# One core, a two-layer hybrid backbone: decay rows read back from memory by SP's queue, rotation by a shuffle, four heads' squares beside each other, modulation's sums as products of rounded parts

## The chip, the cores and the metric

The kernel runs on 1 core of one Trainium2 chip. The metric is the device time of one execution in microseconds (us). The engines are named as in the profile: PE is TensorE (matrix products; PEld its weight loads), DVE is VectorE, ACT is ScalarE, POOL is GpSimd, SP is SyncE, which here only issues DMAs.

## The reference

Two layers over 256 latent and 256 context tokens of 1024 channels, float32. Each layer modulates its input, runs two token mixers on one combined projection, and then a mixture of 16 experts. What the change touches, cut:

```python
m_lat = jnp.split(jax.nn.silu(c) @ mod_w[l] + mod_b[l], 6, axis=-1)      # shift, scale, gate, twice; m_ctx alike
...
def rope_2d(x, cos, sin):                 # on q and k of the attention branch, latent tokens
    x1, x2 = xs[..., 0, :], xs[..., 1, :]
    out = jnp.stack([x1 * c - x2 * s, x2 * c + x1 * s], axis=-2)
...
q = l2_normalize(q.reshape(B, L, G_HEADS, G_KEY_DIM))    # DeltaNet branch; k alike
...
gcum = jnp.cumsum(chunk3(g), axis=-1)     # g: log decay, per token, head and direction
decay = jnp.exp(jnp.where(causal, gcum[..., :, None] - gcum[..., None, :], -jnp.inf))
a_mat = jnp.where(strict, jnp.einsum('nbhid,nbhjd->nbhij', kb, kc) * decay, 0.0)
sol = lax.linalg.triangular_solve(a_mat + jnp.eye(CHUNK), rhs, ...)
qk = jnp.where(causal, jnp.einsum('nbhid,nbhjd->nbhij', qc, kc) * decay, 0.0)
```

## The kernel before

The program is written as some hundred strands (Python generators: `modulation`, `conv_worker`, `norms`, `build`, `double`, `scan`, `att_worker`, `attend`, the expert strands). A planner (`Scheduler`) takes one operation after the other from the strands, by costs written in the code and by a table of priorities (`PRIO`), and writes each engine's instructions in that order; on the chip each engine runs its list in order and waits on semaphores. All weight loads go through SP's list. Buffers come from pools: 20 pages (128 x 2048 numbers), 16 `t5` (128 x 512), 14 `tiny`, and the 8 PSUM banks. An operation that finds no buffer makes its strand wait.

The places that the change and the prediction's steps touch:

- Decay rows. `decay_gates` makes `GC`, the sums of the log decays, with the token on the partition. The difference of two sums needs a row as well: `grow` makes it by four transposes on PE (one for each head) of a column repeated 128 times, into a bank. `build(t)` needs such rows for each of 4 tiles and 2 directions to make A; `double(t, d)` inverts I + A by blocks (products of 32 x 32 and 64 x 64 pieces), and then needs the same rows again for P, the decayed products of q and k, in the place where A stood. `scan` waits for P by `p_ev`.
- Squares. Behind each head's short convolution, `conv_worker` squares the head (ACT) and sums over the 128 channels, which lie on the partitions, by one product with a column of ones for each tile, into `Y.sqs`, a bank held by the whole layer's DeltaNet branch. `norms` copies them out for the root.
- Rotation. In `att_worker` a product with a permutation matrix (`K["perm"]`) swaps each 16 rows with the next 16; then come two multiplications and an addition on DVE.
- Modulation. `modulation` multiplies SiLU(c) with 512 columns of weights in four groups of 32 rows of PE beside each other, and sums the four partial results by a product with a 0/1 matrix (`sel2`), in float32. For the gates and the second shift and scale (`kind >= 2`) that product is 2 x 512.

A product of float32 numbers stands in the trace as two records, one of numbers rounded to `F32R` as one, a transpose as one. A float32 weight matrix is used as a rounded part and the rest (`split`), in three products (`mm3`).

## Time and profile before

| | us |
|---|---|
| median of 3 runs (lowest, highest) | 1632.36 (1616.32, 1634.97) |
| the profiled execution | 1628.14 |
| its span, first to last instruction | 1626.0 |
| PE busy in it | 1493.8 |
| DVE busy | 931.7 |
| ACT busy | 535.8 |

The span falls into stretches: until about 600 us the dense part of the first layer (modulation, projections, DeltaNet, attention, merging), to about 960 its routing and experts, to about 1320 the dense part of the second layer, then routing and the experts of that layer. Every time below is counted from the start of the span. A busy share is read within one stretch; the granted clock of PE stands beside it as a share of full speed.

### The profile page before, as it was taken

How to read it: one execution, taken by the hardware profiler on the slowest of the kernel's cores; microseconds unless marked ns; L12 is line 12 of the kernel's file. 1: busy time of each engine (PE TensorE's matmuls, PEld its weight loads, DVE VectorE, ACT ScalarE, POOL GpSimd, SP SyncE). 2: the span in 40 equal slices, each digit the busy share in tenths (PEclk: the TensorE clock that was granted, in tenths of full speed). 3: DMA queues.
4: the chain of work that ended last, by engine and by line, in shares of the span. 5: the costliest groups of instructions: out<-in, count | busy, mean ns of one | idle time of the engine just before them, and what ended most of it. 6: DMA issues, size and time to landing. Idle time of an engine off the chain costs nothing. (4 is left out here: it accounts for less than half of the span.)

```text
span 1626.0 us, 24829 instructions
## 1 busy us (share of the span) xinstructions
PE 1493.8 (92%) x9551; PEld 1017.6 (63%) x9552; DVE 931.7 (57%) x2391; ACT 535.8 (33%) x950; POOL 63.1 (4%) x84
## 2 busy tenths in 40 slices
PE   5999999999999977999999899999999957999974
PEld 2776788756787843465564367788889844454421
DVE  1677945768437586365575966792778666210023
ACT  2533343434331121264553253343554302110110
POOL 1000000000000001111010000000000000000000
PEclk9999999999999997999998999996999977999988
DMA  9415522152336577799998743440055955899994
GB/s 312 158 53 175 160 57 80 50 210 91 117 130 249 190 302 283 277 422 403 417 383 326 260 151 109 156 102 5 28 182 176 312 218 214 304 421 421 420 408 203
DMA packets 147725, 363.17 MB, mean 223 GB/s; under 512 B 27932, under 2 KB 82284, under 8 KB 122256
## 3 DMA queue, kind: packets, MB, share of 16 engines
q1 hardware_dynamic: 139808, 342.91, 56.9%
q0 software_dynamic: 6512, 16.38, 3.0%
q10 hardware_dynamic: 1280, 2.23, 0.4%
q8 instruction: 77, 1.26, 0.3%
q14 instruction: 48, 0.39, 0.1%
HBM read 345.47 MB, written 21.56 MB: 226 GB/s over the span
## 5 line engine op out<-in xcount | busy, mean ns | idle before, releaser
L451 PE MATMUL bank<-page,page 128*128 128x512 f32 (+3 forms) x3776 | 733.7, 349 | 13.5 <-ACT page L485 6.5
L451 PEld LDWEIGHTS bank<-page,page 128*128 128x128 f32 (+2 forms) x3776 | 567.6, 189 | 126.1 <-issue 27.3
L489 DVE TENSOR_TENSOR page<-page,page 128x1024 fp32r<-128x1024 f32 (+3 forms) x219 | 250.8, 1164 | 96.9 <-ACT page L485 94.9
L485 ACT ACTIVATE page<-page 128x1024 fp32r<-128x1024 f32 (+1 forms) x196 | 200.3, 1046 | 122.8 <-PE bank L451 65.8
L463 PE MATMUL bank<-page,t 128*64 128x512 f32 (+2 forms) x736 | 208.9, 607 | 6.8 <-DMA page<-in_w_exp_dram 5.9
L485 ACT ACTIVATE t<-bank 128x512 f32<-128x512 f32 (+5 forms) x168 | 79.8, 480 | 306.7 <-PE bank L468 210.5
L489 DVE TENSOR_TENSOR t<-bank,t 128x512 f32<-128x512 f32 (+3 forms) x63 | 49.6, 792 | 188.0 <-PE bank L463 153.8
L485 ACT ACTIVATE page<-bank 128x512 f32<-128x512 f32 (+2 forms) x127 | 70.2, 557 | 222.1 <-PE bank L451 97.9
L463 PE MATMUL bank<-page,page 128*32 128x512 f32 (+2 forms) x512 | 136.0, 604 | 8.0 <-DMA page<-in_w_exp_dram 7.6
L463 PEld LDWEIGHTS bank<-page,t 128*64 128x64 f32 (+2 forms) x736 | 64.6, 147 | 103.4 <-issue 87.1
L451 PE MATMUL bank<-t,page 32*32 32x16 f32 (+4 forms) x1472 | 117.1, 244 | 2.1 <-DVE t L504 1.8
L451 PEld LDWEIGHTS bank<-t,page 128*128 128x128 f32 (+3 forms) x1472 | 104.9, 160 | 18.9 <-issue 11.3
L468 PE MATMUL bank<-cf,t 128*128 128x128 f32 (+2 forms) x468 | 79.1, 287 | 36.0 <-DVE t L489 25.9
L468 PEld LDWEIGHTS bank<-cf,t 128*128 128x128 f32 (+2 forms) x468 | 54.8, 144 | 70.6 <-DVE t L489 31.8
L463 PEld LDWEIGHTS bank<-page,page 128*32 128x32 f32 (+2 forms) x512 | 47.0, 144 | 81.2 <-issue 67.1
L451 PE MATMUL bank<-page,csil 128*32 128x512 f32 x384 | 68.0, 678 | 17.2 <-DMA page<-in_mod_w_dram 16.5
L451 PE MATMUL bank<-page,t 128*128 128x512 f32 (+2 forms) x392 | 81.4, 346 | 2.1 <-DVE page L489 1.1
L451 PEld LDWEIGHTS bank<-page,t 128*128 128x128 f32 (+1 forms) x392 | 56.0, 185 | 26.4 <-issue 9.2
L518 DVE SCALAR_TENSOR_TENSOR t<-bank,tiny,t 128x508 f32<-128x508 f32 (+3 forms) x96 | 66.5, 700 | 7.5 <-ACT t L480 6.4
L480 ACT ACTIVATE t<-bank,tiny 128x512 f32<-128x512 f32 (+1 forms) x72 | 44.6, 623 | 53.5 <-PE bank L451 27.8
L480 ACT ACTIVATE page<-page 128x512 f32<-128x512 f32 (+2 forms) x44 | 25.6, 588 | 84.1 <-DVE page L489 48.5
L468 PE MATMUL bank<-cf,page 128*128 128x128 f32 (+1 forms) x248 | 41.7, 305 | 9.9 <-DMA page<-h_dram,cd 8.4
(178 smaller groups left out, 1139.7 us busy)
## 6 DMA issues: line engine op xcount, KB each, us to landing
page<-in_w_exp_dram SPq DMA_DIRECT2D x192, 1024.0 KB
page<-in_mod_w_dram SPq DMA_DIRECT2D x48, 1024.0 KB
page<-in_w_in_dram SPq DMA_DIRECT2D x44, 1024.0 KB
page<-in_w_o_dram SPq DMA_DIRECT2D x8, 1024.0 KB
y_dram<-t POOLq DMA_DIRECT2D x6, 1024.0 KB, 8.3
page<-m_dram SPq DMA_DIRECT2D x12, 512.0 KB
page<-y_dram SPq DMA_DIRECT2D x6, 1024.0 KB
page<-in_w_pb_dram SPq DMA_DIRECT2D x4, 1024.0 KB
```

The lines of the kernel that those rows point to most:

```text
L451: lambda: PE.matmul(o, a, b, start=start, stop=stop, skip_group_check=True))], [o], [a, b])
L463: PE.matmul(o, a, b, start=start, stop=stop, skip_group_check=True)
L468: SC.rec([("PE", 0.11, lambda: PE.transpose(o, a, idn))], [o], [a])
L480: SC.rec([("ACT", acte(width(o), in_psum(a)), lambda: S.activation(o, a, f, bias=bias, scale=scale, **k))], aps(o, accum_out), aps(a, bias ...
L485: SC.rec([("ACT", acte(width(o), in_psum(a)), lambda: S.activation(o, a, AF.Copy, bias=0.0, scale=1.0)), ("DVE", dve(width(o), in_psum(a), ...
L489: opts = [("DVE", dve(width(o), in_psum(a) or in_psum(b)), lambda: V.tensor_tensor(out=o, in0=a, in1=b, op=op)), ("POOL", 0.1 + width(o) * ...
L518: lambda: V.scalar_tensor_tensor(o, a, s, b, op0=op0, op1=op1, **k))],
```

## The change

In `build`, the rows of the sums come from memory: `decay_gates` transposes `GC` once, copies it and writes it to `gc_dram` (32 x 128 numbers); for every two tiles one DMA reads all 16 rows back into the page of A, each to all 128 partitions. For P, `double` reads the four rows of a tile and direction again, into the place of A, once it is done with A (`sum_rows`), and a strand of its own, `decayed`, makes P from them. `conv_worker` keeps its squared head in a `t5`; `norms` multiplies a 128 x 32 block of ones with the squares of four heads, each on 32 columns of PE's array beside the others, copies the bank, and brings the sums to tokens by a product with a 0/1 matrix for each tile. The rotation swaps rows by DVE's shuffle. The sums of modulation with `kind >= 2` are two products of rounded parts with a 0/1 matrix of 16 columns.

```diff
@@ modulation
-            cpy(part, bk)
+            if kind < 2:
+                cpy(part, bk)
+            else:
+                lo_ = yield "t5"
+                split(pt_.r(512), lo_.r(512), bk)
...
-                mm(bk[:2, :], K["sel2"], part, True, True)
-                tt(part[:2, :], bk[:2, :], br, OP.add)
-                dma(m_dram[l, :, i * 512:(i + 1) * 512], part[:2, :], "ACT")
+                mm(bk[:16, :], sel2r, pt_.r(512), True, False)
+                mm(bk[:16, :], sel2r, lo_.r(512), False, True)
+                tt(br, bk[:2, :], br, OP.add)
+                SC.free(lo_)
+                dma(m_dram[l, :, i * 512:(i + 1) * 512], br, "ACT")
@@ conv_worker
                 act(a4, dst, AF.Square)
-                for t in range(2 * ns):
-                    mm(Y.sqs[:, 1 - part, 2 * s0 + t, hd:hd + 1], a4[:, t, :], ones[:, 0:1], True, True)
+                Y.sq[part, hd] = a_
@@ norms
+        b = yield "bank"
+        n0 = 256 if Y.last and part == 0 else 0
+        mm_beside([b.v(512)[32 * hd:32 * hd + 32, n0:] for hd in range(4)], [ones[:, :32]] * 4,
+                  [Y.sq[part, hd].v(512)[:, n0:] for hd in range(4)], True, True)
+        st = yield "t5"
+        cpy(st.v(512)[:, n0:], b.v(512)[:, n0:])
+        SC.free(b, *(Y.sq.pop((part, hd)) for hd in range(4)))
+        w, w2, b = yield ("tiny", "tiny", "bank")
...
+        for t in range(n0 // 128, 4):
+            mm(b.v(4, 16)[:, t], st.v(4, 128)[:, t], K["selH"], True, True)
+        vcopy(shaped(sq, (4 - n0 // 128, 4)), b.v(4, 16)[:, n0 // 128:, :4])
@@ decay_gates
+        b, rows_ = yield ("bank", "t5")
+        tr(b.v(128)[:32], gv[:, 6, :])
+        cpy(rows_.v(128)[:32], b.v(128)[:32])
+        dma(dram(gc_dram[l], 0, [[128, 32], [1, 128]]), rows_.v(128)[:32])
+        SC.free(b, rows_)
@@ in place of grow
+    def sum_rows(Y, t, d):
+        dma(cell(Y.pA, t, d).rearrange("p h j -> p (h j)"),
+            dram(gc_dram[Y.l], (t * 8 + d * 4) * 128, [[0, 128], [1, 512]]))
@@ build
+        if t % 2 == 0:
+            dma(Y.pA[si].v(2048), dram(gc_dram[Y.l], si * 2048, [[0, 128], [1, 2048]]))
+            SC.set(Y.gc_ev[si])
+        yield Y.gc_ev[si]
...
-            A = cell(Y.pA, t, d)
-            b = yield "bank"
-            gr = grow(Y, b, t, d)
+            A = gr = cell(Y.pA, t, d)
@@ double, behind the inverse
-                b = yield "bank"
-                gr = grow(Y, b, t, d)
...
+                sum_rows(Y, t, d)
+    def decayed(Y, groups):
+        for t, d in groups:
+            if t not in Y.tiles:
+                continue
+            yield Y.u_ev[t, d]
+            for hd in range(4):
+                yield Y.conv_ev[0, hd]
+            A = cell(Y.pA, t, d)
+            for hd in range(4):
+                stt(A[:, hd], A[:, hd], hcol(Y.GC, t, d, hd), capP[:, d], OP.subtract, OP.min)
...
@@ att_worker
-                b = yield "bank"
-                mm(b.v(256), K["perm"], lat, True, True)
-                tt(tmp.v(256), b.v(256), K["sin"], OP.mult)
-                SC.free(b)
-                tt(lat, lat, K["cos"], OP.mult)
-                tt(lat, lat, tmp.v(256), OP.add)
+                SC.rec([("DVE", dve(256, False), lambda o=tmp.v(256), a=lat:
+                         V.stream_shuffle(out=o, in_=a, mask=[c ^ 16 for c in range(32)]))], [tmp.v(256)], [lat])
+                tt(tmp.v(256), tmp.v(256), K["sin"], OP.mult)
+                tt(tmp.v(256, o=256), lat, K["cos"], OP.mult)
+                tt(lat, tmp.v(256, o=256), tmp.v(256), OP.add)
```

The table of priorities stays as it was (`decayed` takes the one of its `double`, plus 0.01). Since the planner works on the new list of operations, the order changes all over. Three places, in the first layer. First SP's list ahead of the first pieces of A that are written out (`blk_dram`); before:

```order
L537 DMA page_317<-in_mod_w_dram 128x4x512
L537 DMA page_800<-in_mod_w_dram 128x4x512
L537 DMA page_1028<-in_mod_w_dram 128x4x512
L537 DMA page_1045<-in_mod_w_dram 128x4x512
L537 DMA page_1083<-in_w_in_dram 128x8x256
L537 DMA page_1097<-in_mod_w_dram 128x4x512
L537 DMA page_1102<-in_mod_w_dram 128x4x512
L537 DMA blk_dram<-page_934 16x16x16 x3
```

The same place of SP's list now:

```order
L538 DMA page_322<-in_mod_w_dram 128x4x512
L538 DMA page_747<-in_mod_w_dram 128x4x512
L538 DMA gc_dram<-t_852 32x128
L538 DMA page_884<-gc_dram 128x2048
L538 DMA page_886<-gc_dram 128x2048
L538 DMA page_910<-in_mod_w_dram 128x4x512
L538 DMA page_1026<-in_mod_w_dram 128x4x512
L538 DMA blk_dram<-page_884 16x16x16 x8
```

The write of the sums and the two reads of 1 MB stand between two loads of modulation weights; the second read, and all behind it, comes after the write has landed.

Further on in SP's list, where the block inverses of the first layer are done, before:

```order
L537 DMA page_1536<-in_w_in_dram 128x8x256
L537 DMA page_1547<-in_w_in_dram 128x8x256
L537 DMA page_1589<-in_mod_w_dram 128x4x512
L537 DMA t_1636<-inv_dram 16x16x16 x2
L537 DMA page_1701<-in_mod_w_dram 128x4x512
```

And there now, with the rows for P (each `page<-gc_dram 128x512` waits for the last product that reads A of its tile and direction):

```order
L538 DMA page_1647<-in_w_in_dram 128x8x256
L538 DMA page_1659<-in_w_in_dram 128x8x256
L538 DMA page_884<-gc_dram 128x512
L538 DMA page_1692<-in_mod_w_dram 128x4x512
L538 DMA page_884<-gc_dram 128x512
L538 DMA page_1848<-in_mod_w_dram 128x4x512
L538 DMA page_884<-gc_dram 128x512
L538 DMA page_1944<-in_w_in_dram 128x8x256
L538 DMA page_884<-gc_dram 128x512
L538 DMA page_886<-gc_dram 128x512 x3
L538 DMA page_2730<-in_mod_w_dram 128x4x512
```

Eight such reads stand among the weight loads, each ahead of the next load.

Last PE's list where `double` works on tiles 2 and 3 of the first layer (the pieces of 32x16, 64x32 and 32x32 are `double`'s, those of 128x256 an attention projection's), before:

```order
L451 MATMUL bank_2518<-t_2448,page_936 128x128 x4
L451 MATMUL bank_2527<-t_2517,page_936 32x16 x16
L451 MATMUL bank_2432<-page_2342,page_115 128x256 x2
L451 MATMUL bank_2432<-page_2342,page_117 128x256
L451 MATMUL bank_2432<-page_2342,page_115 128x256 x2
L451 MATMUL bank_2554<-t_2517,t_1636 32x16 x16
L451 MATMUL bank_2432<-page_2342,page_117 128x256
L451 MATMUL bank_2391<-t_2265,t_1636 32x16 x13
L451 MATMUL bank_2415<-page_2250,page_114 128x256 x2
L451 MATMUL bank_2587<-t_2517,page_936 64x32 x8
```

And now:

```order
L452 MATMUL bank_2214<-t_2205,page_886 32x16 x16
L452 MATMUL bank_2217<-t_2203,page_886 32x16 x16
L452 MATMUL bank_2245<-t_2205,t_1370 32x16 x16
L452 MATMUL bank_2265<-t_2203,t_1370 32x16 x16
L452 MATMUL bank_2275<-page_1649,page_118 128x256 x2
L452 MATMUL bank_2285<-t_2205,page_886 64x32 x8
L452 MATMUL bank_2299<-t_2203,page_886 64x32 x8
L452 MATMUL bank_2275<-page_1649,page_120 128x256
L452 MATMUL bank_2275<-page_1649,page_118 128x256 x2
L452 MATMUL bank_2323<-t_2205,t_1370 32x32 x8
```

Both directions run at once, and fewer products of the projection stand between their small pieces.

## Rows read from the trace of the kernel before

**Rows 1.** The page: busy us of each engine, share of the span, instructions.

```profile
PE 1493.8 (92%) x9551; PEld 1017.6 (63%) x9552; DVE 931.7 (57%) x2391; ACT 535.8 (33%) x950; POOL 63.1 (4%) x84
```

**Rows 2.** Windows by stretch: length, busy of PE, PEld, DVE, ACT, POOL, clock, DMA share, GB/s.

```profile
40.00:600.00 560.00, 544.66 (x3867) 418.25 (x3860) 364.14 (x944) 199.78 (x386) 12.50 (x18) 0.99 0.42 140
...
640.00:960.00 320.00, 302.22 (x1363) 167.04 (x1361) 199.93 (x380) 139.42 (x189) 25.48 (x27) 0.96 0.86 336
960.00:1320.00 360.00, 351.15 (x3032) 299.29 (x3032) 244.08 (x624) 144.72 (x282) 6.71 (x12) 0.95 0.45 148
...
1360.00:1600.00 240.00, 226.78 (x973) 97.17 (x973) 48.65 (x155) 32.30 (x55) 6.98 (x7) 0.98 0.97 395
```

**Rows 3.** Groups of instructions by form, PE: removed kinds (busy us, mean ns, idle before).

```profile
L468 PE MATMUL bank<-cf,t 128*128 128x128 f32 x456 | 77.2, 288 | 29.6 <-DVE t L489 25.9 <-DVE t L518 2.0 <-DVE tiny L518 1.2
...
L451 PE MATMUL bank<-t,cf 128*2 128x512 f32 x32 | 16.3, 592 | 2.4 <-ACT t L485 2.4
...
L451 PE MATMUL bank<-ones,t 128*128 128x1 f32 x112 | 13.8, 242 | 0.2 <-ACT t L480 0.2
...
L451 PE MATMUL bank<-page,cf 128*128 128x256 f32 x32 | 10.2, 399 | 0.0
```

**Rows 4.** Timeline of PE: one of each removed kind, and what starts next.

```profile
77.66 0.95 PE L451 MATMUL bank<-ones,t 128*128 128x1 f32 x8
78.46 1.88 PE L451 MATMUL bank<-page,page 128*128 128x512 f32 x7
...
153.82 1.02 PE L451 MATMUL bank<-t,cf 128*2 128x512 f32 x2
154.78 0.70 PE L451 MATMUL bank<-page,cf 128*128 128x256 f32 x2
155.12 1.05 PE L451 MATMUL bank<-page,page 128*128 128x512 f32 x3
...
1087.92 0.60 PE L468 MATMUL bank<-cf,t 128*128 128x128 f32 x4
1088.28 1.91 PE L451 MATMUL bank<-page,page 128*128 128x256 f32 x14
```

**Rows 5.** Timeline of PE: the nearest to each added kind, and what starts next.

```profile
66.77 11.05 PE L451 MATMUL bank<-page,page 128*16 128x512 f32 x48
...
964.79 0.52 PE L451 MATMUL bank<-t,cf 128*128 128x16 f32 x4
965.16 0.39 PE L451 MATMUL bank<-t,ones 128*128 128x32 f32 x2
...
1414.83 3.64 PE L463 MATMUL bank<-page,page 128*32 128x512 f32 x32
1418.40 1.98 PE L463 MATMUL bank<-page,t 128*128 128x512 f32 x4
```

**Rows 6.** Groups of instructions by form, DVE.

```profile
L518 DVE SCALAR_TENSOR_TENSOR page<-bank,t,cb 128x128 f32<-128x128 f32 x112 | 31.7, 343 | 8.4 <-PE bank L468 8.1
...
L489 DVE TENSOR_TENSOR page<-t,page 128x512 fp32r<-128x512 f32 x26 | 17.5, 690 | 12.6 <-ACT page L485 9.3 <-ACT page L480 3.2
...
L518 DVE SCALAR_TENSOR_TENSOR t<-t 128x128 f32<-128x128 f32 x24 | 6.8, 288 | 0.8
...
L489 DVE TENSOR_TENSOR page<-page,cf 128x256 f32<-128x256 f32 x16 | 6.6, 413 | 0.0
```

**Rows 7.** Windows around the second layer's block inverses, columns as in rows 2.

```profile
1080.00:1098.00 18.00, 17.76 (x299) 16.53 (x297) 16.12 (x52) 9.11 (x22) 0.52 (x1) 1.00 0.32 81
1098.00:1128.00 30.00, 30.00 (x317) 25.65 (x316) 4.40 (x12) 10.91 (x32) 1.05 (x2) 0.50 0.05 6
```

**Rows 8.** Waits: who waited for whom, us in total, times, longest.

```profile
SPq L537 <- PE bank L451: 492.9, 60, 49.4
...
SPq L537 <- DMA inv_dram<-t: 27.4, 4, 9.3
...
ACT page L485 <- DMA page<-in_w_in_dram: 23.0, 8, 10.7
```

More of the change, by code (lines that the diff above doesn't have):

```diff
@@ L78, in const_layout @@
     blk["ident"] = (r == c)
-    blk["perm"] = (r == (c ^ 16))
     f = np.float32
@@ L97, in const_layout @@
     blk["selR"] = (q[:, None] == np.arange(16)[None, :])
+    blk["selH"] = (p[:, None] == 32 * np.arange(16)[None, :])
     blk["neg16"] = np.where(q < 16, -1.0, 0.0)[:, None]
@@ L420, in tile_kernel @@
     inv_dram = [dp.tile([128, 256], F32, name=f"inv{i}_dram") for i in range(2)]
+    gc_dram = [dp.tile([32, 128], F32, name=f"gc{l}_dram") for l in range(2)]
     sizes = {"page": 2048, "t5": 512, "tiny": 32}
@@ L457, in mm3, with mm_beside @@
         mm(o, a[1], b[0], False, stop)
-    def mm_beside(os, as_, bs, start, stop):
+    def mm_beside(os, as_, bs, start, stop, rate=600):
         def f():
@@ L463, in f @@
                 PE.matmul(o, a, b, start=start, stop=stop, skip_group_check=True)
-        SC.rec([("PE", width(bs[0]) / 600 + 0.008 * len(os), f)], list(os), [*as_, *bs])
+        SC.rec([("PE", width(bs[0]) / rate + 0.008 * len(os), f)], list(os), [*as_, *bs])
     def tr(o, a, idn=None):
@@ L591, in tile_kernel @@
     capP = shaped(K["capP"], (2, 128))
+    sel2t = sb.tile([128, 16], F32, name="sel2t")
+    sel2r = sel2t[:, :].bitcast(F32R)
+    V.tensor_copy(sel2r, K["selR"])
     ones = sb.tile([128, 128], F32, name="ones")
@@ L997, in gdn_begin @@
         Y.rn = Y.gv[:, 12:14, 0:16].rearrange("p k (t h) -> p k t h", t=4)
-        Y.sqb = yield "bank"
-        Y.sqs = Y.sqb.v(2, 4, 4)
+        Y.sq = {}
         SC.set(Y.gdn_ev)
@@ L1043, in conv_worker @@
                 cpy(Y.vtok[:, :, hd, :], tb.v(4, 128))
-                SC.free(tb)
-            SC.free(a_)
+                SC.free(tb, a_)
             SC.set(Y.conv_ev[part, hd])
@@ L1052, in norms @@
             yield Y.conv_ev[part, hd]
-        w, w2 = yield ("tiny", "tiny")
-        o = 8 if Y.last and part == 0 else 0
+        b = yield "bank"
[6 more added lines that the diff above has]
+        w, w2, b = yield ("tiny", "tiny", "bank")
+        o = n0 // 32
         sq, z = w.v(16)[:, o:], w2.v(16)[:, o:]
-        vcopy(sq, Y.sqs[:, 1 - part].rearrange("p a b -> p (a b)")[:, o:])
+        for t in range(n0 // 128, 4):
+            mm(b.v(4, 16)[:, t], st.v(4, 128)[:, t], K["selH"], True, True)
+        vcopy(shaped(sq, (4 - n0 // 128, 4)), b.v(4, 16)[:, n0 // 128:, :4])
+        SC.free(b, st)
         rsqrt(Y.gv[:, 13 - part, o:16], sq, 1.0, z)
@@ L1156, in hrow @@
         return bc(v[:, t, d * 4:d * 4 + 4], 128)
-    def grow(Y, b, t, d):
-        for hd in range(4):
-            tr(b.v(4, 128)[:, hd, :], hcol(Y.GC, t, d, hd).to_broadcast([128, 128]))
-        return b.v(4, 128)
+    def sum_rows(Y, t, d):
+        dma(cell(Y.pA, t, d).rearrange("p h j -> p (h j)"),
+            dram(gc_dram[Y.l], (t * 8 + d * 4) * 128, [[0, 128], [1, 512]]))
     def chunk_pages(Y):
@@ L1313, in double @@
             SC.free(b, wt)
-            SC.set(Y.u_ev[t, d])
             Y.di_left[si] -= 1
@@ L1318, in double @@
             if t in Y.tiles:
-                for hd in range(4):
-                    yield Y.conv_ev[0, hd]
-                b = yield "bank"
-                gr = grow(Y, b, t, d)
-                for hd in range(4):
-                    stt(A[:, hd], gr[:, hd], hcol(Y.GC, t, d, hd), capP[:, d], OP.subtract, OP.min)
-                SC.free(b)
-                act(A, A, AF.Exp)
-                b = yield "bank"
-                for hd in range(4):
-                    mm(b.v(4, 128)[:, hd], Y.kq(hd)[:, t, 0, :], Y.kq(hd)[:, t, 1, :], True, True)
-                tt(A, A, b.v(4, 128), OP.mult)
-                SC.free(b)
+                sum_rows(Y, t, d)
+            else:
+                SC.set(Y.p_ev[t, d])
+            SC.set(Y.u_ev[t, d])
+    def decayed(Y, groups):
[8 more added lines that the diff above has]
+                stt(A[:, hd], A[:, hd], hcol(Y.GC, t, d, hd), capP[:, d], OP.subtract, OP.min)
+            act(A, A, AF.Exp)
+            b = yield "bank"
+            for hd in range(4):
+                mm(b.v(4, 128)[:, hd], Y.kq(hd)[:, t, 0, :], Y.kq(hd)[:, t, 1, :], True, True)
+            tt(A, A, b.v(4, 128), OP.mult)
+            SC.free(b)
             SC.set(Y.p_ev[t, d])
@@ L1521, in att_worker @@
                 lat = dst[:, i, 256 - m0:]
-                b = yield "bank"
-                mm(b.v(256), K["perm"], lat, True, True)
-                tt(tmp.v(256), b.v(256), K["sin"], OP.mult)
-                SC.free(b)
-                tt(lat, lat, K["cos"], OP.mult)
-                tt(lat, lat, tmp.v(256), OP.add)
+                SC.rec([("DVE", dve(256, False), lambda o=tmp.v(256), a=lat:
[3 more added lines that the diff above has]
+                tt(lat, tmp.v(256, o=256), tmp.v(256), OP.add)
                 SC.free(tmp)
@@ L2433, in open_layer @@
         Y.pu_ev = [Event(f"pu{i}") for i in R2]
+        Y.gc_ev = [Event(f"gc{i}") for i in R2]
         Y.blk_ev = [Event(f"blk{i}") for i in R4]
@@ L2475, in open_layer @@
         sp(norms(Y, 0), 4, "normq")
-        sp(sq_end(Y), 2, "sqe")
         sp(chunk_pages(Y), 2.7, "pt")
@@ L2484, in open_layer @@
             sp(double(Y, [(a + 1, 1), (a, 1)]), 2.76 + .02 * si, f"dbl{si}b")
+            for n, o in enumerate(([(a, 0), (a + 1, 0)], [(a + 1, 1), (a, 1)])):
+                SC.spawn(decayed(Y, o), PRIO[f"{Y.l}dbl{si}{'fb'[n]}"] + .01, f"dec{si}{'fb'[n]}")
         for d in R2:
```

4 lines of the change are left out of this document (removed).

## The prediction

> **What bounds the kernel now.** I read the page first: PE is busy for 1493.8 of 1626.0 us, DVE for 931.7 [rows 1]. A mean over stages says little, so the windows by stretch come next [rows 2]. In the dense part of the first layer PE is busy for 544.66 of 560 us, in that of the second for 351.15 of 360; DVE (364.14, 244.08) and the DMA engines (0.42, 0.45) are not full there. The expert stretches have DMA shares of 0.86 and 0.97, the second of them at 395 GB/s: their length follows from the weights. So the dense parts are PE's, and since every expert needs the routing that follows them, a microsecond off PE's list there moves the end by one, as long as PE doesn't start to wait. The waits that are left in them are small: 15.3 and 8.9 us. All that the change takes from PE stands in the dense parts but for a few pieces between 918 and 955 us, where PE works too.
>
> The price of a PE instruction is read from the timeline as the distance from its start to the start of the next kind, not as its duration: instructions overlap. The groups by form give a transpose 288 ns [rows 3], while four of them hold PE for only 0.36 us [rows 4].
>
> The Trainium skill, page "Perfetto Trace Analysis", section "Identifying the Most-Contended Engine", says that the busy share of matmuls is no good measure of how far PE is from its limit, because they are pipelined, and wants weight loads looked at as well. The trace agrees: the same transposes' durations add up to over three times the time that they hold PE. By durations alone the change would remove some 91 us and add some 41, a gain of 50; I go by starts.
>
> **What PE loses.** Numbers of instructions come from the code and the order.
> - 112 transposes for the rows: 16 groups of four in `build` (4 tiles, 2 directions, 2 layers) and 12 in `double`. Four hold PE from 1087.92 to 1088.28 [rows 4]: 28 x 0.36 = 10.1 us.
> - Squares: eight records (four products) from 77.66 to 78.46, 0.80 us a head [rows 4]; 12 heads in full and 4 half ones (the last layer's q): 14 x 0.80 = 11.2 us.
> - Sums of modulation: two records from 153.82 to 154.78, 0.96 us [rows 4], 16 of them: 15.4 us.
> - Rotation: two records from 154.78 to 155.12 [rows 4], 16 x 0.34 = 5.4 us.
> Together 42.1 us.
>
> **What PE gets.**
> - 32 products of rounded parts, 16 columns of weights by 512: 48 records of a like kind start within 66.77 to 77.66 [rows 4, 5], 0.227 us each: 7.3 us.
> - Three sets of four products beside each other and one half set. 32 such records, four experts beside each other, take 1414.83 to 1418.40 [rows 5], 0.11 each; a set is eight records, 0.89 us: 3.1 us.
> - 14 products of 128 x 16 behind them: two (four records) take 964.79 to 965.16 [rows 5]: 14 x 0.185 = 2.6 us. Two transposes of 32 columns, 0.2.
> Together 13.2 us. **PE's balance is 42.1 - 13.2 = 28.9 us less.**
>
> **DVE** is not the bound, so its changes cost nothing while PE's full list covers them. The shuffle has no row; the nearest is the product of two pages of 128x256, 413 ns [rows 6], 16 of them 6.6 us (with half and double that, 3 and 13). The Trainium skill, page "VectorE: DVE Perf Modes", section "The perf-mode tier table", gives a shuffle of 2048 columns some 2400 ns at the plain rate; scaled by columns that is an estimate of 0.3 us here, 4.8 in all, and would leave the sum as it is; no run here shows it yet. The rests of the split sums are 16 subtractions of 128x512 at 690 ns, 11.0 us; the 112 operations on rows read a page in place of a bank, about 288 in place of 343 ns [rows 6], 6.2 us less. In all some 11 us more of 931.7. It is fullest just ahead of the second layer's block inverses, 16.12 of 18 us, and even there PE works 17.76 [rows 7]. ACT gets four copies of a bank and two small ones, under 3 us.
>
> **Memory.** Four reads of 1 MB and 12 of 256 KB are 7 MB; at 395 GB/s [rows 2] 18 us of transfer, in stretches in which the DMA engines are more than half idle. They cost nothing in throughput. Their latency is longer than four transposes: the second layer's and the first's rows wait for the write to land. SP waited for the landing of the four writes of block inverses 27.4 us, 6.9 each [rows 8]; with the read as much again at most, `build` starts 10 to 14 us later in each layer. What hides it is the work of the other strands on PE, the projections of attention above all; without it PE would stand still for up to 2 x 14 us. I take nothing, since PE had other work in nearly all of both dense parts.
>
> **Waits that are added on SP.** Its list is in order, so a read that waits holds every weight load behind it. The two reads of 1 MB in the first layer hold a load of modulation weights for the 6.9 us of the write; the 12 reads for P wait for `double`. The planner puts them where it expects no wait. I take nothing here too; the price if that is wrong is a rival below.
>
> **Buffers.** A bank less is held through the DeltaNet branch, and 28 takes of a bank fall away; but up to eight `t5` of 16 hold squares until all four heads are there. A gain is bounded by PE's waits in the dense parts, 24 us; what more waits could cost is not in the trace, and I bound it by the same 24 us. I take none.
>
> **Sum.** 1628.1 - 28.9 = 1599.2, against the profiled execution, which stands 4.2 us below the median of the runs and inside their span (1616 to 1635). I forecast 1600 us; the sum is not better than that, as PE's prices have some 10% on either side, 4 us.
>
> **The rivals.**
> - *The clock falls in the first layer too.* In the second layer the granted clock stood at 0.50 of full speed (1.2 in place of 2.4 GHz) for 30 us, while PE's row still reads 30.00 of 30 busy [rows 7]; ahead of it PE had begun the small pieces of `double`, two directions at once. In the first layer before, many products of 128x256 stood between those pieces, and the mean clock from 40 to 600 us was 0.99 [rows 2]. Now both directions run together on tiles 2 and 3, with few between. A stretch like that of 30 us costs up to 15: 1606 to 1615. Against it: the stretch is shorter here and soon followed by larger products.
> - *The clock stays up in the second layer.* The same pieces in another order might pass without the fall: 1599 - 15 = 1584. For it: the order there is new; against it: it still opens with both directions of a pair.
> - *PE isn't the bound after all.* If latency (rows through memory, squares kept until the fourth head, norms in two steps) sets the pace of the DeltaNet chain, part or all of the 29 us turns into waits, down to nothing gained: 1612 to 1628. Against it: PE's 97 and 98% in the dense parts. That the change doesn't do what it says would end here too; the order shows that it does.
> - *SP's list.* SP waited 60 times for PE, 8.2 us each [rows 8]. If each of the 12 reads for P held the list for as long, the load behind it would come 8 us later. Weight pages have little to spare: 8 of them already came late for the split on ACT, by 23.0 us [rows 8]. If half of the 12 reach PE, 6 x 8.2 = 49 us: 1599 + 49 = 1648, slower than before. It decides from the point at which a read's wait is longer than the lead of the load behind it. Against it: the planner orders SP by the same plan that orders PE.
>
> **How the numbers follow.** Forecast 0.48 (1588 to 1610, half of it below the bound named next), clock falls in the first layer 0.15, clock stays up in the second 0.13, absorbed 0.13, SP's list 0.11. A difference of 2%, 32.6 us, is about what a measurement of this kernel can tell from no change. Below 1632.4 - 32.6 = 1599.7 lie half of the first case and the third: 0.24 + 0.13, with a little of the buffers' gain 0.39. Slower by over 2% (above 1665) is a third of SP's case, 0.04. The range, 1582 to 1632, takes in all cases but SP's and the far ends of the third.
>
> **What would show it.** PE's transposes fewer by 112, records of `ones` by 128x1 gone; two records of 128*16 at about 0.23 us from start to start where one product of 0.96 was; the dense parts shorter by some 17 and 12 us with PE as full as before; the expert stretches unchanged. Wrong is the sum if PE's idle time in the dense parts grows over 24 us, with waits on DMA of `gc_dram` or of weights behind it; the clock's cases show as 0.5 between 200 and 300 us, or none about 1080 us. SP's case shows as waits of SP at the new reads, followed by late weights on ACT.

## The result and the profile after

The changed kernel takes 1632.73 us in the median of 19 runs (1627.94 to 1644.76), the kernel before 1624.7 (1612.76 to 1637.06): a ratio of 1.0061, with a 95% interval of 1.0037 to 1.0085. No gain of 29 us came; it is slightly slower, and 0.7 us above the range. The two profiled executions stand closer together (1628.85 against 1628.14 us, spans 1627.1 and 1626.0), so rows of theirs can place the 29 us that are missing, but not all of the 8 us between the medians.

The page of the kernel after, busy time of each engine, as in [rows 1]:

```profile
PE 1467.7 (90%) x9357; PEld 1000.8 (62%) x9358; DVE 951.3 (58%) x2446; ACT 536.0 (33%) x950; POOL 62.7 (4%) x84
```

PE's list did get shorter, by 26.1 us of busy time. The windows of the kernel after, columns as in [rows 2]:

```profile
40.00:600.00 560.00, 528.14 (x3686) 410.98 (x3686) 370.07 (x959) 197.67 (x380) 12.61 (x18) 0.95 0.42 140
...
640.00:960.00 320.00, 297.28 (x1295) 161.71 (x1294) 198.80 (x368) 134.78 (x181) 26.49 (x28) 0.96 0.87 340
960.00:1320.00 360.00, 336.56 (x2968) 286.97 (x2966) 256.98 (x672) 149.70 (x293) 6.65 (x12) 0.94 0.49 161
...
1360.00:1600.00 240.00, 226.33 (x964) 96.15 (x963) 47.68 (x151) 31.72 (x54) 6.98 (x7) 0.98 0.97 396
```

What PE lost as work it got back as idle time: over the whole span it stands still for 159.4 us, 27.2 more than the 132.2 of the kernel before. In the two dense windows it is 31.9 + 23.4 = 55.3 us, where it was 15.3 + 8.9 = 24.2 in [rows 2]; these windows leave out one long wait of the kernel before, which is shown below. The clock of the first window fell from 0.99 to 0.95. The second expert stretch is as before.

The clock is lower over whole runs as well. Its mean was 0.929 to 0.941 of full speed in the 19 runs of the changed kernel, and 0.945 or more in every run of the kernel before that stands beside an experiment below. The time of the kernel before goes with it: in the 23 runs beside e13 to e15, from 1636.53 us at 0.945 to 1615.19 at 0.963. That the clock is the cause of this is not shown.

Where each layer's dense part ends can be read from one wait: at the routing PE stands still for 6.4 us (in the second layer 6.7) for a tile of DVE named `Mb`. The row of PE's timeline in the kernel before, first layer, and then the one after (start, duration, operation, in brackets the idle time ahead of it and who ended it):

```profile
608.70 0.22 PE L451 MATMUL bank<-Mb,cb 128*128 128x16 bf16 x2 [6.44 <-DVE Mb L489]
```

```profile
618.24 0.22 PE L452 MATMUL bank<-Mb,cb 128*128 128x16 bf16 x2 [6.42 <-DVE Mb L490]
```

The first layer is 9.5 us longer. In the second that row starts at 1352.79 before and at 1352.18 after: counted from the first, 744.1 and 733.9 us. There 10.2 us were gained, but not on PE's list. The second layer of the kernel before ends in a wait that [rows 2] don't show, since they stop at 1320 us and go on at 1360: ahead of the last transposes before the routing, PE stands still for 18.0 us for DVE. In the changed kernel it is 3.2 us. PE, DVE and SP before:

```profile
1335.48 1.12 PE L468 MATMUL bank<-cf,t 128*128 128x128 f32 x4 [18.01 <-DVE t L489]
...
1322.50 1.30 DVE L489 TENSOR_TENSOR bank<-bank,page 128x512 f32<-128x512 f32 x2 [10.83 <-DMA page<-m_dram]
...
1299.86 6.06 SPq L537 DMA_DIRECT2D page<-in_w_exp_dram  x5
1306.27 0.33 SPq L537 DMA_DIRECT2D page<-m_dram  x1
```

And PE and SP after:

```profile
1331.02 1.12 PE L469 MATMUL bank<-cf,t 128*128 128x128 f32 x4 [3.19 <-DVE t L490]
...
1305.32 0.33 SPq L538 DMA_DIRECT2D page<-m_dram  x1
1307.06 8.18 SPq L538 DMA_DIRECT2D page<-in_w_exp_dram  x5
```

Before, a page that DVE needs (`m_dram`) is read behind five loads of expert weights, and DVE starts its steps towards the last norm at 1322.50, 5 us after the end of PE's last product; after, it is read ahead of them, and DVE starts these steps at 1315.01, while PE still works. Up to this wait the second layer is as long as before (708.8 and 709.6 us from the first routing). The wait follows from the order and not from the change: e11 below, which has none of the change, waits 3.2 us there, and e7, which has all of it, 17.7.

The start of the routing row, and the time from the first to the second, are given below for every kernel, as "routing 1" and "to routing 2".

Where did the first layer lose? Three windows of 20 us of it and one of the second layer, of the kernel after, and then two of the same of the kernel before:

```profile
140.00:160.00 20.00, 9.62 (x31) 4.14 (x32) 16.15 (x63) 4.73 (x7) 0.98 (x2) 0.66 0.78 229
160.00:180.00 20.00, 17.78 (x210) 13.86 (x208) 14.79 (x48) 4.56 (x10) 1.51 (x3) 0.91 0.49 134
180.00:200.00 20.00, 20.00 (x115) 15.54 (x114) 10.42 (x19) 8.43 (x16) 0.00 (x0) 0.74 0.22 58
1040.00:1060.00 20.00, 8.44 (x53) 5.35 (x52) 19.89 (x76) 5.20 (x9) 0.99 (x2) 0.76 0.36 81
```

```profile
140.00:160.00 20.00, 20.00 (x104) 11.83 (x104) 16.52 (x50) 8.37 (x12) 0.00 (x0) 1.00 0.73 223
1040.00:1060.00 20.00, 20.00 (x120) 16.25 (x117) 16.02 (x48) 8.16 (x13) 0.00 (x0) 1.00 0.30 101
```

From 140 to 160 us PE works 9.62 of 20 us, from 1040 to 1060 only 8.44, and the clock is down there or behind it. DVE is well filled in both places (16.15 and 19.89), but in the kernel before as well (16.52 and 16.02); what differs is what it does there, and who waits for it. The timeline of the kernel after shows it. PE:

```profile
135.85 1.92 PE L452 MATMUL bank<-page,csil 128*32 128x512 f32 x16
145.09 0.61 PE L452 MATMUL bank<-t,sel2t 128*16 128x512 f32 x1 [7.32 <-ACT t L486]
147.10 0.61 PE L452 MATMUL bank<-t,sel2t 128*16 128x512 f32 x1 [1.40 <-DVE t L530]
149.93 2.17 PE L452 MATMUL bank<-page,page 128*128 128x512 f32 x4 [2.22 <-ACT page L486]
...
1055.43 0.61 PE L452 MATMUL bank<-t,sel2t 128*16 128x512 f32 x1 [8.21 <-ACT t L486]
```

ACT, the same kernel (L481 is the exponential of A, L486 a copy, here the rounded part of the sum that PE waits for):

```profile
140.81 0.63 ACT L481 ACTIVATE page<-page 128x512 f32<-128x512 f32 x1 [0.42 <-DVE page L519]
143.93 0.63 ACT L481 ACTIVATE page<-page 128x512 f32<-128x512 f32 x1 [2.49 <-DVE page L519]
...
144.46 0.58 ACT L486 ACTIVATE t<-bank 128x512 fp32r<-128x512 f32 x1
```

And DVE:

```profile
127.02 1.13 DVE L519 SCALAR_TENSOR_TENSOR page<-page,t,cb 128x128 f32<-128x128 f32 x4
129.21 1.13 DVE L519 SCALAR_TENSOR_TENSOR page<-bank,t,page 128x128 f32<-128x128 f32 x4 [1.06 <-ACT page L481]
130.25 2.18 DVE L519 SCALAR_TENSOR_TENSOR page<-page,t,cb 128x128 f32<-128x128 f32 x8
...
142.76 1.13 DVE L519 SCALAR_TENSOR_TENSOR page<-page,t,cb 128x128 f32<-128x128 f32 x4
```

From 127 to 144 us DVE does nearly all 64 operations of `build` on end (the last four stand at 144.59). The rows of all four tiles are there at once, and `build` has a strong priority (a low number, 1.465). ACT's list is in order: the copy for modulation's sum stands behind eight exponentials, each of which needs four of DVE's subtractions first. PE's list is in order too, and its next product is that sum. Before, four transposes on PE and a bank stood ahead of every four subtractions, which spread `build`'s work over PE's other products.

### The profile page after: what moved, and what is told of

Same layout as the page of the kernel before. It is cut to its first block, busy times and chain, and to the rows that moved or that the text cites. A ratio compares the mean times of both kernels' runs of the same rounds, so it can differ in the third digit from the quotient of the medians.

```text
span 1627.1 us, 24559 instructions
## 1 busy us (share of the span) xinstructions
PE 1467.7 (90%) x9357; PEld 1000.8 (62%) x9358; DVE 951.3 (58%) x2446; ACT 536.0 (33%) x950; POOL 62.7 (4%) x84
## 5 line engine op out<-in xcount | busy, mean ns | idle before, releaser
L452 PEld LDWEIGHTS bank<-page,page 128*128 128x128 f32 (+2 forms) x3776 | 574.0, 191 | 132.2 <-issue 26.8
L486 ACT ACTIVATE page<-page 128x1024 fp32r<-128x1024 f32 (+1 forms) x194 | 198.6, 1046 | 137.1 <-PE bank L452 64.3
L486 ACT ACTIVATE t<-bank 128x512 f32<-128x512 f32 (+7 forms) x173 | 81.8, 478 | 310.7 <-PE bank L469 181.5
L490 DVE TENSOR_TENSOR t<-bank,t 128x512 f32<-128x512 f32 (+3 forms) x79 | 60.5, 771 | 193.0 <-PE bank L464 150.6
L486 ACT ACTIVATE page<-bank 128x512 f32<-128x512 f32 (+2 forms) x127 | 70.2, 555 | 211.8 <-PE bank L464 84.0
L452 PE MATMUL bank<-t,page 128*128 128x128 f32 (+4 forms) x1472 | 118.0, 246 | 7.3 <-DVE t L501 2.6
L452 PE MATMUL bank<-page,csil 128*32 128x512 f32 x384 | 69.8, 710 | 23.8 <-DMA page<-in_mod_w_dram 23.7
L469 PE MATMUL bank<-cf,t 128*128 128x128 f32 (+3 forms) x358 | 61.6, 288 | 21.9 <-DVE t L490 8.0
L469 PEld LDWEIGHTS bank<-cf,t 128*128 128x128 f32 (+3 forms) x358 | 42.0, 145 | 51.5 <-issue 19.4
L519 DVE SCALAR_TENSOR_TENSOR t<-bank,tiny,t 128x508 f32<-128x508 f32 (+3 forms) x96 | 66.1, 699 | 12.5 <-ACT t L481 11.4
L481 ACT ACTIVATE t<-bank,tiny 128x512 f32<-128x512 f32 (+1 forms) x72 | 44.7, 625 | 59.5 <-DVE tiny L505 36.0
L490 DVE TENSOR_TENSOR page<-page,bank 128x512 f32<-128x512 f32 x50 | 33.8, 682 | 29.3 <-PE bank L452 23.8
L481 ACT ACTIVATE page<-page 128x512 f32<-128x512 f32 (+2 forms) x44 | 25.9, 591 | 74.7 <-DVE page L490 44.3
```

The lines of the kernel that those rows point to most:

```text
L452: lambda: PE.matmul(o, a, b, start=start, stop=stop, skip_group_check=True))], [o], [a, b])
L469: SC.rec([("PE", 0.11, lambda: PE.transpose(o, a, idn))], [o], [a])
L481: SC.rec([("ACT", acte(width(o), in_psum(a)), lambda: S.activation(o, a, f, bias=bias, scale=scale, **k))], aps(o, accum_out), aps(a, bias ...
L486: SC.rec([("ACT", acte(width(o), in_psum(a)), lambda: S.activation(o, a, AF.Copy, bias=0.0, scale=1.0)), ("DVE", dve(width(o), in_psum(a), ...
L490: opts = [("DVE", dve(width(o), in_psum(a) or in_psum(b)), lambda: V.tensor_tensor(out=o, in0=a, in1=b, op=op)), ("POOL", 0.1 + width(o) * ...
L519: lambda: V.scalar_tensor_tensor(o, a, s, b, op0=op0, op1=op1, **k))],
```

## The experiments

Each was timed beside the kernel before on the same chip. The chips differ between the groups e1 to e4, e5 to e8, e9 and e10, e11 and e12, and e13 to e15, and the median of the kernel before with them (1627.4, 1629.1, 1624.0, 1623.0 and 1624.0 us), so kernels of different groups are compared by their ratios. The last two columns are of one profiled execution each; the first layer of e14 is that of the kernel before, unchanged, and came out 4.4 us longer, so differences of that size say little.

| | median us | ratio to before (95%) | routing 1 | to routing 2 |
|---|---|---|---|---|
| before | 1624.7 | | 608.7 | 744.1 |
| changed | 1632.7 | 1.0061 (1.0037 to 1.0085) | 618.2 | 733.9 |
| e1 sums only | 1639.9 | 1.0084 (1.0047 to 1.0122) | 619.1 | 741.5 |
| e2 squares only | 1640.7 | 1.0098 (1.0060 to 1.0137) | 612.4 | 740.7 |
| e3 rotation only | 1677.4 | 1.0334 (1.0282 to 1.0385) | 628.5 | 763.6 |
| e4 rows only | 1658.0 | 1.0209 (1.0160 to 1.0259) | 622.1 | 757.6 |
| e5 before, reordered | 1642.9 | 1.0099 (1.0070 to 1.0129) | 630.5 | 743.4 |
| e6 before, reordered | 1640.6 | 1.0077 (1.0046 to 1.0107) | 628.2 | 744.9 |
| e7 build last | 1623.5 | 0.9980 (0.9948 to 1.0012) | 604.8 | 737.1 |
| e8 table refitted | 1611.3 | 0.9906 (0.9873 to 0.9939) | 597.1 | 743.1 |
| e9 build 0 last | 1623.4 | 0.9986 (0.9946 to 1.0025) | 613.1 | 726.6 |
| e10 stalls filled | 1643.3 | 1.0130 (1.0082 to 1.0179) | 614.9 | 749.1 |
| e11 before refitted | 1619.9 | 1.0000 (0.9972 to 1.0029) | 608.9 | 735.9 |
| e12 clock held | 1601.6 | 0.9869 (0.9826 to 0.9912) | 595.8 | 733.5 |
| e13 changed, held | 1635.8 | 1.0059 (1.0029 to 1.0089) | 618.4 | 736.9 |
| e14 before, held | 1626.4 | 1.0009 (0.9976 to 1.0043) | 613.1 | 734.9 |
| e15 held with half | 1600.4 | 0.9855 (0.9811 to 0.9898) | 600.0 | 730.0 |

**Each part alone (e1 to e4).** The kernel before with one of the four parts of the diff. The main lines of e3, the smallest, cut:

```diff
-                mm(b.v(256), K["perm"], lat, True, True)
-                tt(tmp.v(256), b.v(256), K["sin"], OP.mult)
+                SC.rec([("DVE", dve(256, False), lambda o=tmp.v(256), a=lat:
+                         V.stream_shuffle(out=o, in_=a, mask=[c ^ 16 for c in range(32)]))], [tmp.v(256)], [lat])
+                tt(tmp.v(256), tmp.v(256), K["sin"], OP.mult)
```

> Only the sums of modulation are changed (PE loses 15.4 us and gets 7.3 us: 8.1 us less). By the theory of the burst (the changed kernel loses its gain where build's 64 operations on DVE come in one row and PE's next product, the sum of modulation, waits behind them through ACT) the rows of build are still made on PE, so there is no such row and the gain shows: 1617 us against 1625, PE's idle time in the dense parts as before (about 24 us). By the theory of the order (the table of priorities belongs to the old list of operations, and whatever changes the list loses PE's cover) nothing shows or it gets slower: 1623 to 1640, with 10 us or more of new idle time.

> Only the squares are changed (PE 5.5 us less). Theory of the burst: 1619 us, idle time as before. Theory of the order: 1623 to 1640.

> Only the rotation is changed (PE 5.4 us less, DVE as much as before within a few us). Theory of the burst: 1619 us. Theory of the order: 1623 to 1640, though nothing but 16 small products has left PE's list. This is the sharpest of the four single parts, since no wait on memory and no long chain comes with it.

> Only the decay rows come from memory (PE 9.9 us less). Theory of the burst: the row of 64 operations on DVE is there, but without the split of the modulation's partial sums PE has no product that waits behind it, or one that waits shorter: 1615 to 1630, and the stall stands ahead of build in each layer. Theory of the order: 1620 to 1640, with the idle time at other places too.

All four are slower, though each takes work from PE; e3 and e4 lie above both ranges that were expected. The theory of the burst alone falls: the rotation brings no row of `build` and no read of memory, and costs 50 us. Four parts that each lose cannot be added up either: together they lose less than any one of them. What they have in common is that the planner makes a new order. e3's second layer, windows:

```profile
980.00:1385.00 405.00, 368.79 (x3046) 309.22 (x3045) 262.77 (x669) 147.51 (x288) 6.71 (x12) 0.87 0.40 132
```

The mean clock is 0.87; in the kernel before it was 0.92 over the like stretch, 960 to 1346.

**The order without the change (e5, e6).** The kernel before, one number of the table moved:

```diff
-"0build0": 1.465
+"0build0": 1.565
```

```diff
-"0attw0": 3.982
+"0attw0": 3.682
```

> The kernel before with one priority moved (0build0 from 1.465 to 1.565): the same products on PE, only in another order. By the theory of the order, an order that the table was not chosen for costs PE idle time and clock though no work is added: 1635 to 1665 us. By the rival (what makes the single parts slower lies in the parts: reads, shuffles, splits, buffers held longer) it is within 5 us of 1625.

> The same with another priority (0attw0 from 3.982 to 3.682). Theory of the order: 1630 to 1660. Rival: within 5 us of 1625.

PE's list holds the same instructions, in another order, and the time rises by 1.0 and 0.8%, 12 to 16 us. This shows that the order alone can cost about half of what is missing. Nearly all of it lies in the first layer. That layer up to its routing, of before, of e5 and of e6:

```profile
40.00:602.00 562.00, 546.21 (x3884) 419.51 (x3877) 364.31 (x945) 200.50 (x387) 12.50 (x18) 0.99 0.42 141
```

```profile
40.00:623.00 583.00, 555.76 (x3883) 431.33 (x3875) 368.14 (x949) 196.70 (x379) 11.69 (x16) 0.96 0.41 135
```

```profile
40.00:621.00 581.00, 559.40 (x3887) 430.11 (x3883) 368.89 (x948) 201.97 (x390) 12.73 (x18) 0.96 0.41 136
```

Of e5's 21 us, 9.6 are PE busy for longer with the same instructions, at a clock of 0.96 in place of 0.99, and 11.4 are idle time (27.2 against 15.8). The profiled executions are the slowest of e5's runs and the second slowest of e6's, so these rows show more than the medians do.

**The burst (e7, e9).** The changed kernel with `build` behind the other strands, in both layers (e7) or for tile 0 of the first (e9):

```diff
-"0build0": 1.465, "0build1": 1.465, "0build2": 1.465, "0build3": 1.465
+"0build0": 7.0, "0build1": 7.1, "0build2": 7.2, "0build3": 7.3
-"1build0": 0.2, "1build1": 0.837, "1build2": 0.837, "1build3": 1.303
+"1build0": 7.0, "1build1": 7.1, "1build2": 7.2, "1build3": 7.3
```

> The changed kernel with the priorities of build alone moved behind the other strands (0build0 to 0build3 and 1build0 to 1build3 from 0.2 to 1.465 to 7.0 to 7.3): all work stays, but DVE serves the attention's and the modulation's operations before the 64 of build. Theory of the burst: the two stretches in which PE stood still ahead of the block inverses (13.6 us about 130 to 165, 11.6 us about 1040 to 1062) go, and the time falls by 10 to 25 us, to 1608 to 1622. By the rival that the rows' latency through memory is what PE waits for, the stalls stay, or grow, since build starts even later: 1633 to 1650.

> The changed kernel with one priority moved: 0build0 from 1.465 to 7.136, so that in the first layer build of tile 0 stands behind the other strands. Theory of the burst: the stall about 130 to 165 us goes and the first layer's dense part ends some 10 us earlier; the second layer keeps its stall about 1047 us (8 us in one piece): 1615 to 1626 us, between the changed kernel (1633) and the one with all of build moved (1623.5). Rival (e7 gained by luck of the order as a whole, not by the stall): no relation to the stalls, 1625 to 1650.

In e7 the ratio is 0.9980, where the changed kernel's is 1.0061, some 13 us; 1623.5 is just above the range that was expected. Both long waits are gone, as its windows show:

```profile
140.00:160.00 20.00, 18.59 (x86) 13.53 (x82) 17.18 (x62) 8.38 (x12) 0.00 (x0) 1.00 0.64 188
...
1040.00:1060.00 20.00, 20.00 (x131) 18.26 (x130) 17.11 (x65) 8.14 (x14) 1.00 (x2) 1.00 0.43 120
```

So PE waited for the place of `build` in DVE's and ACT's lists, not for the rows' way through memory: in e7 the first rows are used 10.0 us after their read is issued (117.87 and 127.86), and in the changed kernel as well (117.03 and 127.02). The two layers bear this out better than the total does. The first layer is 13.4 us shorter than the changed kernel's. The second is 3.2 us longer, but there the wait at its end is back, with 17.7 us in place of 3.2; without it the layer would be 11.3 us shorter. The two stalls had been put at 13.6 and 11.6 us.

e9 keeps the second layer's stall (8.1 us) and gains as much in all; its first layer gains 5 us of the 10 that were expected, and its second 7.3, with the stall still in it. The two moves change the rest of the order too, so a price for one stall can't be read from them.

**Tables of their own (e8, e11).** Entries of the table moved at random, a move being kept when the planner's list ended earlier: 14 for the changed kernel, 52 (and a longer search) for the kernel before. Five of e8's 14:

```diff
-"0build0": 1.465, "0build1": 1.465, "0inv1": 1.411, "1attw1": 3.21, "1conv0": 3.122
+"0build0": 7.136, "0build1": 2.001, "0inv1": 0.879, "1attw1": 6.577, "1conv0": 4.224
```

> The changed kernel with a table of priorities chosen anew for its own list of operations (14 entries moved at random and kept where the planner's own list ended earlier; 0build0 from 1.465 to 7.136 among them). Theory of the order: PE's 29 us less come through when the order fits: 1592 to 1612 us. Rival (the operations themselves bring new waits as large as the gain): 1620 to 1635.

> The kernel before with a table of priorities searched in the same way for its own list, for longer (52 entries moved; the planner's own end comes 10 us earlier than with the old table). If a search of this kind gives any list some 15 us, it stands at 1610 us, like the changed kernel with its own table, and the change is then worth nothing. If the table was already fitted to this list and the 15 to 20 us of the refitted changed kernel are the change's own, it stays at 1615 to 1630.

The changed kernel falls to 0.9906; for the kernel before a longer search found nothing, so its table already fitted it about as well as such a search can. With a table of its own to each, the changed kernel is 0.9% faster, about half of the 29 us. That is one order each, and e5 and e6 moved by as much through the order alone: that this is what the change itself is worth is likely, but not shown.

**The clock (e10, e12 to e15).** e10 fills the two stalls of the changed kernel; e12 to e15 put products that nobody needs ahead of the groups of 32x16 pieces in `double`, in the second layer (e13 in both): e12 and e15 in e8's kernel, e13 in the changed kernel, e14 in the kernel before. No order changes, and no result.

```diff
+            for _ in range({0: 120, 14: 130}.get(sums[0], 0)):      # e10, ahead of sums 0 and 14
+                PE.matmul(bk[:, :128], ones_bf, ones_bf, start=True, stop=True, skip_group_check=True)
```

```diff
+            for _ in range(8):                                      # e12 to e14; 4 in e15
+                PE.matmul(bank, ones_bf, ones_bf, start=True, stop=True, skip_group_check=True)
```

> The changed kernel in its own order, with 120 and 130 products of 128 columns (ones by ones, overwritten at once) put on PE ahead of the two sums of modulation for which it waits 7.3 and 8.2 us: work that nobody needs, in time in which PE stands still. If the stalls cost more than their own length because the granted clock falls behind them (0.66 to 0.91 of full speed from 140 to 200 us, 0.61 to 0.90 from 1040 to 1120), the time falls by 5 to 20 us, to 1613 to 1628, with the clock at 1.00 there. If the clock doesn't matter (PE waits for the same results later anyway), it stays at 1633, or rises by up to 3.

> The refitted changed kernel in its own order, with eight products of 128 columns that nobody needs ahead of each of 16 groups of small pieces (32x16) of double in the second layer: about 7 us of work put into the stretch of about 1065 to 1100 us, in which the granted clock was 0.5 to 0.6 while PE was busy. If the clock's fall is the cost of that stretch (up to 17 us) and comes from its small pieces, the clock rises there and the time falls by 3 to 10 us, below 1611. If the pieces' own latency sets the pace there, or the clock falls all the same, it rises by up to 7 us.

> The changed kernel in its own order with the same filling ahead of double's groups of 32x16 in both layers (about 7 us of work that nobody needs in each). If the clock's falls behind double's pieces are a large part of what it lost, the half-clock stretches about 265 to 275 and 1085 to 1109 us go and the time falls from 1633 by 3 to 12 us, to 1621 to 1630; those from 142 to 156 and 1050 to 1064 us, behind the stalls, stay. If the stalls alone are the loss, it rises by 5 to 14 us, by the filling.

> The kernel before in its own order with the filling in the second layer only, where its one long half-clock stretch stands (1098 to 1129 us). If holding the clock is worth as much there as in the refitted changed kernel (10 us): 1613 to 1616, and the clock's cost was in the kernel before as well. If the fall comes from something else there, it rises by up to 7 us.

> The refitted changed kernel with four products ahead of each group in place of eight. If the clock holds with half the filling, 1598 to 1601 us; if it falls again, 1605 to 1615.

e10 missed on the other side. The filling sits in the idle time (6.87 of 7.4 us), and the clock stays at 1.00 through it. It falls just behind, in the next two waits of PE (1.61 us ahead of 146.59, 2.09 ahead of 149.10), and further on a new fall appears where the changed kernel had 1.00. e10's timeline and windows:

```profile
137.18 6.87 PE L815 MATMUL bank<-ones_bf 128*128 128x128 bf16 x120
144.58 0.41 PE L817 MATMUL bank<-t,sel2t 128*16 128x512 f32 x1 [0.52 <-ACT t L486]
```

```profile
136.00:144.00 8.00, 8.00 (x132) 6.83 (x124) 8.00 (x34) 2.48 (x5) 0.00 (x0) 1.00 0.28 37
148.00:156.00 8.00, 6.46 (x18) 2.86 (x18) 6.40 (x20) 1.99 (x2) 0.06 (x1) 0.58 0.81 225
...
140.00:160.00 20.00, 13.82 (x104) 8.07 (x102) 16.36 (x63) 4.35 (x6) 0.98 (x2) 0.78 0.80 234
...
1160.00:1180.00 20.00, 19.82 (x213) 13.93 (x212) 10.61 (x25) 9.57 (x27) 0.00 (x0) 0.71 0.21 67
```

In the second filled place it is alike: 0.98 from 1040 to 1060 us, where the changed kernel had 0.76, and 0.85 in the 20 us behind, where that had 0.90. So filling the two long waits moves the fall and doesn't take it away. Among `double`'s pieces it can be held. Windows of e8, then of e12, in the same order:

```profile
1070.00:1080.00 10.00, 10.00 (x112) 8.14 (x113) 0.91 (x2) 2.77 (x8) 0.00 (x0) 0.50 0.11 12
1080.00:1090.00 10.00, 10.00 (x140) 8.77 (x140) 2.36 (x6) 4.36 (x14) 0.00 (x0) 0.50 0.01 2
```

```profile
1070.00:1080.00 10.00, 10.00 (x227) 8.51 (x224) 1.51 (x4) 4.90 (x14) 0.00 (x0) 1.00 0.14 15
1080.00:1090.00 10.00, 10.00 (x128) 8.88 (x128) 3.58 (x9) 5.46 (x16) 2.04 (x4) 1.00 0.01 2
```

A clock of 0.50 becomes 1.00, and it stays there in e15 as well, with half the filling. The second layer is 9.6 us shorter in e12's profile and 13.1 in e15's. By the ratios e12 and e15 are 0.4 and 0.5% below e8, 6 and 8 us, with intervals that overlap; the mean clock was 0.938 to 0.950 in e8's runs and 0.950 to 0.964 in theirs. So that the clock rises is shown, that it pays is likely. In the changed kernel's own order (e13) and in the kernel before (e14) nothing is gained over the runs, though e14's profile shows the same at 1.00, with the second layer 9.2 us shorter:

```profile
1098.00:1128.00 30.00, 30.00 (x501) 27.14 (x499) 9.49 (x28) 11.07 (x32) 1.05 (x2) 1.00 0.04 5
```

The filling is not free: eight products hold PE for 0.55 us (1061.37 to 1061.92 in e12), some 9 us in each layer. e13, with 18 us of it, takes no longer than the changed kernel (1.0059 and 1.0061), and the median of the mean clock of its runs is 0.947 in place of 0.935. Since PE has little idle time at those places (28.26 of 30 us busy from 1080 to 1110 in the changed kernel), the clock should have given back about what the filling cost; that is an argument from these rows and was not tested. How often the clock falls in the unprofiled runs is not recorded by place. e15 and e12, at 0.9855 and 0.9869, are the fastest kernels here and can't be told apart.

## Why the prediction was wrong

- **PE's list** came out nearly as counted, 26.1 us of busy time less for the 28.9 that were taken, part of it at a lower clock. Transposes with 128 columns went from 456 [rows 3] to 344, the records of `ones` by 128x1 are gone, and from start to start the new rows cost what was taken: 0.23 us for a product of a rounded part (160.24 to 160.47), 1.00 for four products beside each other (0.89 taken). The rows of groups by form, after:

```profile
L469 PE MATMUL bank<-cf,t 128*128 128x128 f32 x344 | 59.1, 290 | 15.8 <-DVE t L490 8.0 <-DVE t L519 4.9 <-DVE tiny L519 2.1
...
L452 PE MATMUL bank<-t,sel2t 128*16 128x512 f32 x32 | 14.1, 467 | 22.6 <-ACT t L486 16.5 <-DVE t L490 4.7 <-DVE t L530 1.4
...
L519 DVE SCALAR_TENSOR_TENSOR page<-page,t,cb 128x128 f32<-128x128 f32 x112 | 31.3, 344 | 10.7 <-DMA page<-gc_dram 10.7
...
L1551 DVE STREAM_SHUFFLE t<-page 128x256 f32<-128x256 f32 x16 | 7.0, 438 | 0.0
```

- **The step that failed** is "a microsecond off PE's list there moves the end by one, as long as PE doesn't start to wait", with DVE's and ACT's changes at nothing "while PE's full list covers them". The condition was the whole question. PE was 97% busy because the order fitted its list; with another list under the same table it stands still for 27.2 us longer, and 42.0 longer if the wait at the second layer's end, shorter by 14.8, is left out. The second row above is the clearest: the 32 products of rounded parts were priced at 7 us, and PE stood still for 22.6 us ahead of them, where it was 2.4 before [rows 3]. Each waits for ACT and for DVE, where one copy was enough before; with the sums alone changed (e1, the row below) that comes to 6.4 us, and with `build` last (e7) to 6.0. So some 4 us are the second wait itself, and the other 16 came with `build`'s burst. I had counted them as PE work and 11 us of DVE, and not as a new wait in an ordered list.

```profile
L451 PE MATMUL bank<-t,sel2t 128*16 128x512 f32 x32 | 13.2, 432 | 6.4 <-DVE t L489 4.1 <-ACT t L485 2.3
```

- **Layer by layer.** I said 17 and 12 us. The first layer gave back all of its 17 and 9.5 more. The 10.2 of the second look like the 12 and are luck: up to the wait at its end nothing was gained. "The waits that are left in them are small: 15.3 and 8.9 us" was a wrong reading, from windows that end at 1320 us, just where a wait of 18.0 us begins.
- **The clock's rivals.** "The clock falls in the first layer too" (0.15) came: from 176 to 190 and from 265 to 275 us PE is nearly full with `double`'s pieces and the products between them, at a clock of 0.52, where the kernel before had 1.00; a third fall, from 142 to 156, belongs to the stall. By the rival's own measure, half of such a stretch, the first two cost up to 12 us. They came on top of the waits, so the time lies above the 1606 to 1615 of that case. In the second layer the clock did not stay up (0.60 from 1080 to 1110).

```profile
176.00:190.00 14.00, 14.00 (x135) 10.09 (x127) 6.08 (x17) 7.13 (x18) 0.00 (x0) 0.52 0.25 48
265.00:275.00 10.00, 9.73 (x135) 8.65 (x132) 3.56 (x13) 5.39 (x18) 0.00 (x0) 0.52 0.15 54
```

- **The other rivals.** "PE isn't the bound after all" (0.13) had the right size with the wrong cause: it named the rows' way through memory, the squares and the norms. The read followed the write by 1.5 us (115.56 to 117.03), where I had put 6.9; the first use came 11.5 us after the write (127.02), within the 10 to 14 that were taken. DVE waited for rows from memory only at P (10.7 us, 6 times, the longest 5.3), not at `build`. "SP's list" (0.11): weights came late for ACT's split 18 times, 46.7 us in all, against 8 times and 23.0 [rows 8]. That was foreseen as a risk; PE's own waits behind such splits, 2.9 us in the first layer, don't make it the cause. PE also waited for modulation weights for 23.7 us in all, before for 16.5, so some 7 us may be SP's; e8, the refitted kernel, has 25.1.
- **DVE's terms.** The rows read from a page cost 344 ns, no less than from a bank [rows 6], so the 6.2 us less did not come, and DVE's busy time rose by 19.6 us in place of 11. The shuffle took 438 ns, near the row that I took (413). The estimate from the Trainium skill, page "VectorE: DVE Perf Modes", section "The perf-mode tier table", was 0.3 us; the measurement decides.
- **What was missing** is a case of its own: the same table, another order. I had written that the order changes all over and gave it no price. e5 and e6 price it at 12 to 16 us for no change in work; e1 to e4 lost 12 to 50 us, for less work on PE.

In the profiles PE's new idle time alone (27.2 us) takes back its shorter list (26.1). What the lower clock costs besides is not settled: the work was done at the slower clock, and waits and falls of the clock stand close together.

## What to carry to other kernels

Where a planner with a fitted table writes the order, a change to the list of operations is measured together with the loss of the fit: move one priority in the old kernel to see how much that can be, and refit both sides before judging the change. Idle time is added up over the whole span first: windows with a gap between them can hide the longest wait of a layer, as here. When work is taken from the busiest engine, look in the new order for what its next instruction waits on: a product that needs two results of other engines in place of one can stand still for longer than it saves. And work that was throttled by the busiest engine (here `build`, by its transposes) can flood another engine once the throttle is gone; its priority has to be looked at again.

## What the runs showed of the hardware

- With PE busy for 30.00 of 30 us and the same order, its clock stood at 0.50 [rows 7] or, with eight products of 128 columns ahead of each group of small pieces, at 1.00 (e14); four did as well (e8 against e15).
- Filling a wait of 7.3 us with products kept the clock at 1.00 through it, but it fell in the next two, of 1.6 and 2.1 us (0.58 from 148 to 156 us). A fall also appeared at 1160 us, though both kernels do the same work in the same order but for the filling.
- A small write to memory and its read back by the same queue: the read was issued 1.5 us after the write.
- DVE reads a 128x128 operand from a page no faster than from a bank: 344 and 343 ns.
